# A decoder layer on one core: its 6328 operations put out along one new table over all engines

## The chip, the core and the metric

The kernel runs on one core of one Trainium2 chip. Five engines matter: TensorE for the matrix products (PE, and PEld for its loads of weights into the array), VectorE (DVE), ScalarE (ACT), GpSimd (POOL) and SyncE (SP). SP only issues transfers; POOL issues transfers too and does a few small copies. The metric is the device time of one execution in microseconds, the median over runs. A second time, the span, is that from the first to the last instruction of one profiled execution.

## The reference

One layer of a decoder for 512 tokens of width 1024, all in float32:

```python
u = rms_norm(h, ln_mix_pre)
proj = u @ w_in                  # qa, ka, va | qb, kb, vb | qm | three gates of 1024 columns
y_swa = swa_sink_attention(...)  # 8 heads of 64, 2 key heads, window 128, sinks, T5 bias
y_sb  = stick_breaking_attention(...)          # 8 heads of 64
y_mem = memory_cross_attention(...)            # 4 heads of 128 over 256 memory rows
g = sigmoid(gates)
merged = g0 * (y_swa @ w_branch_swa) + g1 * (y_sb @ w_branch_sb) + g2 * (y_mem @ w_branch_mem)
h = h + rms_norm(merged @ w_out, ln_mix_post)
u = rms_norm(h, ln_ffn_pre)
a = silu(u @ w_gate) * (u @ w_up)              # 2816 columns each
h = h + rms_norm(a @ w_down, ln_ffn_post)
```

In stick-breaking attention a query gives key s the weight beta_s times the product of (1 - beta) over the keys between s and itself.

## The kernel before, in words

*Arithmetic.* A float32 product is made of three products of the kind fp32r (`mm3`): high by high, high by low, low by high. Every operand therefore comes in two parts. `split` makes them: ACT copies the value to the high part (`hi`), then DVE subtracts that from the value (`lo`). Weights come by DMA in blocks of 128 by 1024 (`raw`; where several blocks are summed, `wide`, `ws0p` to `ws2p` and others, partly summed by the DMA itself), are split, and are read by PE. Large projections (gates, branches, gate and up, down) are computed by seven products in place of eight, with sums of blocks formed ahead on DVE, on ACT and by accumulating DMAs, and with sums of results behind (`gp`, `hp`, `seven_*`, `q_*`, `g_*`, `dn_*`).

*Stages.* First x is loaded, gained, split and squared, and the first four weight blocks are loaded in pieces (`first_load`, `first_split`); the sum of squares goes through two products with ones (`rstd_of`: `sh_x`, `sl_x` are the two parts, `on_x` the ones). Then come the projections for the keys, queries and values, the memory's keys and values, the stick-breaking heads (`sb_head`: scores, two sigmoids `bw` and `br`, a scan over the keys on DVE; `sb_turn`: transposes of the weights by products with `c_ident`; `sb_out`: half-array products of the transposed weights `at` with 64 columns of values, two heads making a pair), the window attention (`swa_pair`, transposed weights `pts`, half-array products as well), the branches, `mix`, the turning of the normalized rows (`turn`, transposes again), the gated up and down products (`gu`, `down`) and the closing norm and sum (`dn_half`: `sqr`, `s`, `fg`, then the `out` transfers).

*Two detours through main memory.* The scan is written in differences of successive values, so the values are needed shifted by one row. `next_values` writes them from `v_all` (a part of the buffer named `wide`) to `rows_v`, 1 MB, and loads them back shifted into four buffers `vnext`, 256 KB each; `value_steps` subtracts these on DVE. `band_bias` makes the bias of the window attention, writes it to `bscr`, 1.5 MB, and loads it back skewed into four buffers `bias`. The transfers of both go through POOL's queue.

*Order.* The generator functions put the operations out in an order of their own, with waits where data or buffers need it. Each engine's operations are noted by a helper (line 232 of the kernel, hence the line of nearly all rows of the profile). At the end of `tile_kernel` a literal `ORDER` with one table per engine is laid over them: each operation of an engine is tied behind the one that its table names before it. These ties are of a class without synchronisation (`NoSync`); they only fix the sequence in which the engine takes its work. Between engines the waits come from data and buffers alone.

*Places.* A second literal, `PLAN`, says for every temporary which of the fixed buffers it takes: four each of `raw`, `hi` and `lo`, 45 single buffers and 14 pairs (`ck`, `ck2`), 16 small ones (`s`), and eight PSUM banks of 512 columns (`p`; `p2` takes two banks as one of 1024). `Places.take` deals them out. A transfer or a product that takes a place waits for the last reader of what was there.

*Waits and tables on ACT.* `table` loads a set of activation functions, and each activation is kept behind the load that it needs.

Of the kernel before, what the change touches and what calls it, by code (L numbers as in the profile page):

```python
# [17 lines left out]
P = 128  # L18
# [19 lines left out]
ORDER = {  # L38
    "tensor": (
# [23 lines left out]
    ),  # L63
    "vector": (
# [81 lines left out]
    ),  # L146
}
PLAN = {
    "raw": (
# [2042 lines left out]
```

## Time and profile before

| | |
|---|---|
| median of 3 runs | 768.73 us (768.61 to 768.78) |
| span of the profiled execution | 766.9 us |
| granted TensorE clock | 0.997 on the mean |
| PE busy | 759.1 us, 99% of the span, 4073 instructions |
| DVE busy | 675.2 us, 88%, 1100 |
| ACT busy | 520.3 us, 68%, 946 |
| POOL busy | 104.1 us, 14%, 140 |
| DMA | 150.06 MB, 196 GB/s on the mean |

The median is the time of whole executions; the profiled one is known by its span, and no other time is given for it. The difference of 1.8 us between the two is what lies around the span. A PE instruction is shown as busy for longer than it keeps the next from starting, so what matters for PE is the distance from one start to the next. "Waits" name, for an engine that stood idle, the work that released it.

### The profile page before, as it was taken

How to read it: one execution, taken by the hardware profiler on the slowest of the kernel's cores; microseconds unless marked ns; L12 is line 12 of the kernel's file. 1: busy time of each engine (PE TensorE's matmuls, PEld its weight loads, DVE VectorE, ACT ScalarE, POOL GpSimd, SP SyncE). 2: the span in 40 equal slices, each digit the busy share in tenths (PEclk: the TensorE clock that was granted, in tenths of full speed). 3: DMA queues.
4: the chain of work that ended last, by engine and by line, in shares of the span. 5: the costliest groups of instructions: out<-in, count | busy, mean ns of one | idle time of the engine just before them, and what ended most of it. 6: DMA issues, size and time to landing. Idle time of an engine off the chain costs nothing.

```text
span 766.9 us, 11497 instructions
## 1 busy us (share of the span) xinstructions
PE 759.1 (99%) x4073; PEld 647.3 (84%) x4073; DVE 675.2 (88%) x1100; ACT 520.3 (68%) x946; POOL 104.1 (14%) x140
## 2 busy tenths in 40 slices
PE   9999999999999999999999999999999999999996
PEld 6789888778888888888888899988888888888885
DVE  7994897799989756999897799899999999999966
ACT  7662677777997758677944596566666668957552
POOL 0303242000222110010001201100000000214000
PEclk9999999999999999999999999999999999999998
DMA  8548999734799895469949958876777746859922
GB/s 277 166 142 233 332 328 254 211 111 149 185 188 192 184 203 163 112 134 210 340 128 329 209 130 240 203 191 180 204 192 203 220 142 187 171 120 216 261 75 111
DMA packets 50170, 150.06 MB, mean 196 GB/s; under 512 B 5984, under 2 KB 7952, under 8 KB 50016
## 3 DMA queue, kind: packets, MB, share of 16 engines
q1 hardware_dynamic: 34224, 94.38, 36.8%
q0 software_dynamic: 15600, 54.80, 36.1%
q8 instruction: 32, 0.52, 0.3%
q14 instruction: 26, 0.21, 0.1%
q10 hardware_dynamic: 288, 0.13, 0.1%
HBM read 140.38 MB, written 19.40 MB: 208 GB/s over the span
## 4 chain that ended last, share of the span: by engine, by line
PE 96%; DMA 1%; DVE 1%; ACT 1%; issue 0%; SPq 0%; DVEq 0%
PE bank L232 96%; DMA xT<-in_xT 1%; DMA raw<-in_w_p 0%; DVE xacc L232 0%; SPq L232 0%; ACT pair L232 0%; DVE pair L232 0%; ACT hi L232 0%; ACT xT L232 0%; DVE lo L232 0%; DVE fg L232 0%; DVE sl_x L232 0%; DVEq L2180 0%; DVE s L232 0%; ACT sqr L232 0%
## 5 line engine op out<-in xcount | busy, mean ns | idle before, releaser
L232 PE MATMUL bank<-pair,hi 128*128 128x512 f32 (+1 forms) x1008 | 254.4, 368 | 0.0
L232 DVE TENSOR_TENSOR lo<-raw,hi 128x1024 fp32r<-128x1024 f32 (+4 forms) x149 | 170.7, 1149 | 36.8 <-ACT hi L232 36.2
L232 PEld LDWEIGHTS bank<-pair,hi 128*128 128x128 f32 x1008 | 177.5, 189 | 27.0 <-ACT hi L232 0.9
L232 ACT CAST hi<-raw 128x1024 fp32r<-128x1024 f32 (+4 forms) x149 | 147.7, 998 | 73.7 <-PE bank L232 54.5
L232 PE MATMUL bank<-hi,pair 128*128 128x512 f32 (+1 forms) x628 | 196.3, 374 | 0.0
L232 PE MATMUL bank<-pair,lo 128*128 128x256 f32 (+1 forms) x752 | 154.7, 302 | 0.0
L232 PEld LDWEIGHTS bank<-hi,pair 128*128 128x128 f32 x628 | 115.3, 188 | 19.5 <-issue 0.2
L232 PEld LDWEIGHTS bank<-pair,lo 128*128 128x128 f32 x752 | 115.6, 190 | 10.9 <-DVE lo L232 0.7
L232 PE MATMUL bank<-lo,pair 128*128 128x512 f32 (+1 forms) x330 | 123.6, 375 | 0.0
L232 ACT CAST hi<-wide 128x1024 fp32r<-128x1024 f32 (+1 forms) x61 | 62.2, 1024 | 27.0 <-PE bank L232 11.3
L232 DVE TENSOR_TENSOR lo<-wide,hi 128x1024 fp32r<-128x1024 f32 (+1 forms) x61 | 71.9, 1185 | 4.6 <-ACT hi L232 4.3
L232 PEld LDWEIGHTS bank<-lo,pair 128*128 128x128 f32 x330 | 62.0, 188 | 10.1
L232 POOL DMA_DIRECT2D raw<-in_w_g x24 | 21.1, 878 | 124.4 <-DVE lo L232 106.2
L232 DVE TENSOR_TENSOR gp<-gp,bank 128x512 f32<-128x512 f32 x49 | 33.6, 687 | 4.6 <-PE bank L232 3.7
L232 ACT ACTIVATE sg<-gp 128x256 f32<-128x256 f32 x42 | 17.7, 421 | 23.0 <-DVE gp L232 22.9
L232 POOL DMA_DIRECT2D raw<-in_w_gu x15 | 13.2, 924 | 147.6 <-DMA raw<-in_w_gu 138.5
L232 ACT COPY gp<-bank 128x512 f32<-128x512 f32 x42 | 24.7, 588 | 2.1 <-DVE aq L232 1.4
L232 DVE TENSOR_TENSOR_SCAN bw<-br,bw 128x512 f32<-128x512 f32 (+3 forms) x32 | 24.6, 809 | 0.2
L232 DVE TENSOR_TENSOR gp<-gp,hp 128x512 f32<-128x512 f32 x36 | 24.7, 685 | 0.0
L232 POOL DMA_DIRECT2D wide<-in_w_gu x12 | 11.2, 934 | 84.6 <-DMA wide<-in_w_gu 76.3
L232 ACT COPY hp<-bank 128x512 f32<-128x512 f32 x36 | 21.5, 598 | 0.0
L232 PE MATMUL bank<-hi,ll 128*128 128x512 f32 x50 | 19.4, 389 | 0.0
(624 smaller groups left out, 1371.8 us busy)
## 6 DMA issues: line engine op xcount, KB each, us to landing
wide<-in_w_gu SPq DMA_DIRECT2D x31, 512.0 KB, 5.1
raw<-in_w_gu SPq DMA_DIRECT2D x26, 512.0 KB, 5.4
raw<-in_w_g POOLq DMA_DIRECT2D x24, 512.0 KB, 6.0
raw<-in_w_g SPq DMA_DIRECT2D x18, 512.0 KB, 4.2
raw<-in_w_gu POOLq DMA_DIRECT2D x15, 512.0 KB, 7.2
raw<-in_w_p SPq DMA_DIRECT2D x14, 512.0 KB, 6.3
wide<-in_w_gu POOLq DMA_DIRECT2D x12, 512.0 KB, 5.8
raw<-in_w_brt SPq DMA_DIRECT2D x9, 512.0 KB, 4.8
```

The source lines that it names most:

```text
L232: ins = f(*args, **kw)
```

## The change

The 6328 operations stay the same: 4009 on PE, 1068 on DVE, 876 on ACT, 136 on POOL, 239 on SP, each with the operands of before. What changes:

1. *How they are put out.* The functions of the kernel now only note operations (`Notes`, `Op`); tensors are described by `View` and made when first used (`once`). At the end `Program.put_out` puts out all operations in the order of one table over all engines, and ties each to the one before it on its engine, as before. The code for ordering without a table (`after`, `behind`, `manual_schedule`, high priorities) is gone.
2. *One table in place of five*, drawn up anew. It fixes the same five sequences, but it also fixes how the operations of different engines are interleaved when the program is built.
3. *PLAN drawn up anew*, with the same number of entries of every kind.

```diff
+class Program:
...
+    def put_out(self, nc, order, follow):
+        real = lambda x: x.real() if isinstance(x, View) else x
+        last, out = {}, set()
+        for n in order or range(len(self.ops)):
+            op = self.ops[n]
+            assert all(b.at in out for b in op.behind)
+            out.add(n)
+            args = [real(x) for x in op.args]
+            ins = getattr(getattr(nc, op.engine), op.name)(*args, **{k: real(x) for k, x in op.kw.items()})
+            if op.engine in last:
+                follow(ins, last[op.engine])
+            last[op.engine] = ins
...
-    for e, text in ORDER.items():
-        seen, last = getattr(nc, e).seen, None
...
-                if last is not None:
-                    follow(seen[k], seen[last])
-                last = k
+    order = []
+    for part in ORDER.split():
+        a, _, b = part.partition("-")
+        order += range(int(a), int(b or a) + 1)
+    program.put_out(tc.nc, order, follow)
```

The new table, three pieces from its first part (641 is the write of `rows_v`, 642 to 645 the loads of `vnext`, 646 the write of `bscr`, 760 to 763 the subtracts that read `vnext`, 781 a scan, 824 the first transpose that reads it):

```
... 652 732-733 715 734-736 698 642 747 749 653 752 ...
... 780 790 778 801 760 802 776 803 865 ...
... 844 817 781 818 843 819-821 856 845 763 824 231 822 ...
```

Laid beside the old tables it comes to this:

- On PE 2985 of the 4009 operations stand at another position, by 6 on the mean and by at most 228; the first 13 and the last 12 stand as before. On DVE 1028 of 1068 stand elsewhere, on ACT 795 of 876, on POOL 92 of 136, on SP 217 of 239.
- The transposes stand in 70 runs on PE; before in 42. The half-array products stand in 7 runs; before in 8, since those of the stick-breaking heads 4 to 7 are now back to back. In all runs, before and after, the two products of a pair of heads or halves stand side by side.
- PE's operations that need a fresh wait on another engine, one that an earlier operation of PE has not waited for already, are 529; before 557.
- In the head, the split of the sum of squares of x is followed on PE by five 512-column products of other work and then by the product of its high part, and two places later by that of its low part; before, the two products stood next to each other with no such work ahead. Some low parts of weights come later, and the order of the first products differs accordingly.
- `rows_v` is written and read nearer to its use. Between the write and the first load of `vnext` stand on PE products of 29 times 512, twice 384 and four times 256 columns; between that load and the subtract that reads it 17 times 512, twice 384, four times 256 columns and ten transposes. Behind that subtract DVE has ten operations up to scan 781, and 25 products of 512 columns stand on PE between the subtract and transpose 824. The write of `bscr` stood right behind that of `rows_v`; it now stands behind it by PE work of some 38 us. The shortest distance from the load of a block by POOL to its split is 25 products of 512 columns.
- The loads and sums of `ws0p` and `ws2p` stand later than before.
- Beside the 384 PE operations that took the 80 us from 300 to 380 us before, the table has 126 DVE operations; before 113.
- The first load of an activation table stands at the 40th position on ACT; before at the 3rd. Copies and squares stand ahead of it, and one table load more is then put into the program ahead of them.
- In the tail the last product for `fg` on DVE stands ahead of the last small `s` operation; before behind it.

More of the change, by code (lines that the diff above doesn't have):

```diff
@@ new lines, with __init__, then, __getitem__ @@
+class View:
+    def __init__(self, make, path=(), shape=None):
+        self.make, self.path, self.shape = make, path, shape
+    def then(self, f):
+        return View(self.make, self.path + (f,))
+    def __getitem__(self, k):
+        return self.then(lambda ap: ap[k])
+    def bitcast(self, dt):
+        return self.then(lambda ap: ap.bitcast(dt))
+    def rearrange(self, *args, **kw):
+        return self.then(lambda ap: ap.rearrange(*args, **kw))
+    def unsqueeze(self, axis):
+        return self.then(lambda ap: ap.unsqueeze(axis))
+    def to_broadcast(self, shape):
+        return self.then(lambda ap: ap.to_broadcast(shape))
+    def real(self):
+        ap = self.make()
+        for f in self.path:
+            ap = f(ap)
+        return ap
@@ new lines, with __init__ @@
+class Op:
+    def __init__(self, at, engine, name, args, kw):
+        self.at, self.engine, self.name, self.args, self.kw = at, engine, name, args, kw
+        self.behind = ()
+class Program:
+    def __init__(self):
+        self.ops = []
+    def put_out(self, nc, order, follow):
[10 more added lines that the diff above has]
+            last[op.engine] = ins
+        assert len(out) == len(self.ops)
@@ L256, in __getitem__, with once, f @@
         return self.held[c]
+def once(make):
+    got = []
+    def f():
+        if not got:
+            got.append(make())
+        return got[0]
+    return f
 class Places:
@@ L396, in tile_kernel @@
     places.open(wp, "wide", 1, [P, 5120])
-    cst = first.enter_context(tc.tile_pool(name="cst", bufs=1))
     places.open(sm, "s", 16, [P, 8])
@@ L412, in dps @@
     def dps(name):
-        return places.take(psd, "p" if PLAN else "d", [P, 512], F32, name)
+        return places.take(psa, "p", [P, 512], F32, name)
     def aps(name):
-        return places.take(psa, "p" if PLAN else "a", [P, 512], F32, name)
+        return places.take(psa, "p", [P, 512], F32, name)
     def banks(name):
@@ L425, in split @@
         ins = nc.scalar.copy(hi, raw)
-        lows = nc.vector.tensor_tensor(lo, raw, hi.bitcast(F32), op=ALU.subtract)
-        if "behind" in st:
-            after(ins, st["behind"][0])
-            after(lows, st["behind"][1])
+        nc.vector.tensor_tensor(lo, raw, hi.bitcast(F32), op=ALU.subtract)
         return ins
@@ L441, in w_split @@
         uid[0] += 1
-        hi = places.take(wp, "hi", [P, 1024], F32R, f"hi{uid[0]}", bufs=4)
-        lo = places.take(wp, "lo", [P, 1024], F32R, f"lo{uid[0]}", bufs=4)
+        hi = places.take(wp, "hi", [P, 1024], F32R, f"hi{uid[0]}")
+        lo = places.take(wp, "lo", [P, 1024], F32R, f"lo{uid[0]}")
         if isinstance(raw, list):
             for i, x in enumerate(raw):
-                ins = split(x[:, :], hi[:, i * 512 : (i + 1) * 512], lo[:, i * 512 : (i + 1) * 512])
+                split(x[:, :], hi[:, i * 512 : (i + 1) * 512], lo[:, i * 512 : (i + 1) * 512])
         else:
-            ins = split(raw[:, :n], hi[:, :n], lo[:, :n])
-        if "chain" in st:
-            after(ins, st["chain"])
+            split(raw[:, :n], hi[:, :n], lo[:, :n])
         return hi, lo
@@ L456, in mm3 @@
         (lh, ll), (rh, rl) = l, r
-        one = nc.tensor.matmul(out, lh, rh, start=start, stop=False, skip_group_check=True)
+        nc.tensor.matmul(out, lh, rh, start=start, stop=False, skip_group_check=True)
         nc.tensor.matmul(out, lh, rl, start=False, stop=False, skip_group_check=True)
-        return one, nc.tensor.matmul(out, ll, rh, start=False, stop=stop, skip_group_check=True)
-    def mm3_behind(*args):
-        one, last = mm3(*args)
-        if "products" in st:
-            after(one, st["products"])
-        st["products"] = last
+        nc.tensor.matmul(out, ll, rh, start=False, stop=stop, skip_group_check=True)
     def mm(out, l, r, start, stop):
@@ L474, in tile_kernel @@
     pin, since = [], []
-    def after(ins, first):
-        if not ORDER:
-            follow(ins, first)
     def follow(ins, first):
@@ L486, in fn @@
         ins = nc.scalar.activation(*args, **kw)
-        for p in pin:
-            after(ins, p)
+        ins.behind = tuple(pin)
         since.append(ins)
@@ L494, in table, with const @@
         ins = nc.scalar.preload_act_table_set(name)
-        for x in since:
-            after(ins, x)
+        ins.behind = tuple(since)
         since.clear()
         pin[:] = [ins]
-    def const(name, shape, pool=cst):
-        t = places.fixed(cst, shape, F32, f"c_{name}") if pool is cst else pool.tile(shape, F32, name=f"c_{name}")
+    def const(name, shape, pool=None):
+        t = pool.tile(shape, F32, name=f"c_{name}") if pool else places.fixed(shape, f"c_{name}")
         nc.sync.dma_start(t[:, :], a[name])
@@ L527, in rstd_of @@
         mm(ps[:, :n], one_t[name], l[:, :n], False, True)
-        rb = places.fixed(cst, [P, n], F32, f"rb_{name}")
+        rb = places.fixed([P, n], f"rb_{name}")
         v, t = ck(f"v_{name}"), ck(f"t_{name}")
@@ L533, in rstd_of @@
         nc.gpsimd.dma_start(row[:, :], rb[:1, :])
-        rs = places.fixed(cst, [P, n // P], F32, f"rs_{name}")
+        rs = places.fixed([P, n // P], f"rs_{name}")
         nc.gpsimd.dma_start(rs[:, :], row[:, :].rearrange("o (t p) -> (o p) t", p=P))
@@ L657, in value_steps @@
         for t, x in enumerate(st.pop("vnext")):
-            after(nc.vector.tensor_tensor(own_values(t), own_values(t), x[:, :], op=ALU.subtract), st["scan"])
+            nc.vector.tensor_tensor(own_values(t), own_values(t), x[:, :], op=ALU.subtract)
     def vcols(t, lo):
@@ L971, in gen @@
                 for k in range(2):
-                    mm3_behind(sbank[i][:, :], seven_left(b, p, k, i), cols((hi, lo), k * 512, 512), first and k == 0, last and k == 1)
+                    mm3(sbank[i][:, :], seven_left(b, p, k, i), cols((hi, lo), k * 512, 512), first and k == 0, last and k == 1)
                 yield 1.36
@@ L1210, in tile_kernel @@
-    pin[:] = [first_table]
+    idle = tc.nc.const_aps.tensor(1.0, [P, 512], BF16)
+    one_t = {}
+    for name in ("x", "m"):
+        one_t[name] = ck(f"on_{name}", F32R)[:, :P]
+        nc.vector.tensor_copy(one_t[name], idle[:, :P])
+    pw = dps("warm")
+    for i in range(WARM):
+        mm(pw[:, :], idle[:, :P], idle[:, :], True, True)
+    first_load(nc.scalar, 0, (0, 2))
+    first_table = nc.scalar.preload_act_table_set("natural_log_exp_and_others")
+    pin[:] = [first_table]
+    load_x(0, 1)
@@ new lines, in tile_kernel @@
+    first_load(nc.sync, 0, (1,))
+    load_x(1, 2)
+    first_load(nc.sync, 1, (0, 1))
+    load_x(2, 3)
+    first_load(nc.sync, 1, (2,))
+    first_load(nc.sync, 2, (0,))
+    load_x(3, 4)
+    first_load(nc.sync, 2, (1, 2))
+    load_x(4, 5)
+    first_load(nc.sync, 3)
+    load_x(5, 8)
+    dn.loaded = dn.have = FIRST
+    for p in range(len(PIECE)):
+        for i in range(FIRST):
+            first_split(i, p)
+        for k in range(*PIECE[p]):
+            gain_split(k)
+    xacc = ck("xacc")
@@ new lines, in tile_kernel @@
+    nc.scalar.activation(xacc[:, :], xraw[0][:, :], AF.Square)
+    for k in range(1, KC):
+        nc.scalar.activation(xraw[k][:, :], xraw[k][:, :], AF.Square)
+        nc.vector.tensor_tensor(xacc[:, :], xacc[:, :], xraw[k][:, :], op=ALU.add)
+    dn.ahead(4, 3)
+    for i in range(FIRST):
+        first_ps[("kb", i)] = aps(f"kb{i}")
+    order = [(i, 0, x) for x in ("hh", "lh", "hl") for i in range(FIRST)]
+    order += [(i, 1, x) for i in range(FIRST) for x in ("hh", "lh", "hl")]
+    for i, k, x in order:
+        w = (his if x[0] == "h" else los)[i]
+        mm(first_ps[("kb", i)][:, :], w[:, k * P : (k + 1) * P], u[k][x[1] == "l"], k == 0 and x == "hh", False)
@@ L1212, in tile_kernel @@
+    gens = [dn.units[i]["mm"](his[i], los[i]) for i in range(FIRST)]
+    for k in range(2, KC + 1):
+        for g in gens:
+            next(g, None)
+    dn.at = FIRST
+    st["rs"], st["rb"] = rstd_of("x", xacc, S, aps)
+    for f in st.pop("waiting"):
+        f()
     ident = const("ident", [P, P], base)
-    sinks = places.fixed(cst, [P, 8], F32, "sinks")
+    sinks = places.fixed([P, 8], "sinks")
     nc.sync.dma_start(sinks[:, :], a["sinks"].to_broadcast([P, 8]))
@@ L1985, in tile_kernel @@
     dn.until(f"branch{MEM}")
-    if PLAN:
-        fp = None
-    else:
-        first.close()
-        fp = ctx.enter_context(tc.tile_pool(name="fp", bufs=9, reuse_waits="tile"))
+    fp = wp
     def f_split(raw, n):
         uid[0] += 1
-        hi = places.take(fp, "fhi", [P, 1024], F32R, f"hi{uid[0]}", bufs=4)
-        lo = places.take(fp, "flo", [P, 1024], F32R, f"lo{uid[0]}", bufs=4)
+        hi = places.take(fp, "fhi", [P, 1024], F32R, f"hi{uid[0]}")
+        lo = places.take(fp, "flo", [P, 1024], F32R, f"lo{uid[0]}")
         if isinstance(raw, list):
@@ L2065, in tile_kernel @@
     kept(1)
-    behind(since[-1], st["mixed"])
     table("silu_and_others")
@@ L2075, in tile_kernel @@
     turn_n2(2)
-    behind(*turn_n2(3))
+    turn_n2(3)
     fs.hold = 6
@@ L2079, in tile_kernel @@
     turn_n22(2)
-    behind(*turn_n22(3))
+    turn_n22(3)
     fs.hold = 8
@@ L2083, in tile_kernel @@
     for t in (2, 3):
-        late = turn_late(t, 0)
-    behind(*late)
+        turn_late(t, 0)
     fs.hold = 10
```

297 lines of the change are left out of this document (99 added, 198 removed), and 423 rows, old and new, of tables (ORDER, PLAN).

## The prediction

> **What bounds the kernel now.** I read the span and the busy shares first, then the list of waits, then the chain that ended last.
>
> ```profile
> span 766.9 us, 11497 instructions
> PE 759.1 (99%) x4073; PEld 647.3 (84%) x4073; DVE 675.2 (88%) x1100; ACT 520.3 (68%) x946; POOL 104.1 (14%) x140
> ...
> PE bank L232 <- PEq L2174: 0.8, 1, 0.8
> PE bank L232 <- DVE sl_x L232: 0.4, 1, 0.4
> ...
> 22.29 737.97 PE bank L232 x3990
> 762.87 0.66 DVEq L2180
> ```
>
> The span is 766.9 us. The median of three runs is 768.73 (768.61 to 768.78), so 1.8 us lie around the span. I add the change's terms to the span and give the result plus 1.8. The list of waits has only two entries for PE, the kernel's start and 0.4 us for sl_x. The chain has one piece of 737.97 us, 3990 matmuls in a row, from 22.29 us to 760.3. An order can therefore win only what lies in the holes of that row, the 22 us before it and the 6 us behind it. The holes are found by the distance between starts, since a matmul's own 0.39 us overlaps the next. Three stretches give the prices; the columns are the stretch, its length, busy time and instructions of PE, its weight loads, DVE, ACT and POOL, the granted clock, the share of the DMA engines and GB/s.
>
> ```profile
> 84.00:90.00 6.00, 6.00 (x30) 4.97 (x29) 5.02 (x10) 4.11 (x8) 1.73 (x4) 1.00 1.04 322
> 300.00:380.00 80.00, 80.00 (x385) 66.72 (x384) 73.02 (x113) 62.13 (x114) 7.03 (x8) 1.00 0.71 189
> 700.00:750.00 50.00, 50.00 (x222) 41.40 (x221) 43.02 (x76) 30.41 (x56) 5.42 (x7) 1.00 0.63 167
> ```
>
> In the late stage 222 matmuls take 50.00 us, 0.225 us each at a granted clock of 1.00: the price of a 512-column matmul with nothing in its way. The other two stretches are used below.
>
> **Head holes.** Against that price I lay the starts of the head.
>
> ```profile
> 4.75 1.02 PE L232 MATMUL bank<-pair,hi 128*128 128x512 f32 x3
> 5.61 0.92 PE L232 MATMUL bank<-pair,lo 128*128 128x512 f32 x3
> 6.36 1.30 PE L232 MATMUL bank<-pair,hi 128*128 128x512 f32 x5
> 7.53 0.50 PE L232 MATMUL bank<-pair,lo 128*128 128x512 f32 x1
> 7.87 0.39 PE L232 MATMUL bank<-pair,hi 128*128 128x512 f32 x1
> ...
> 21.54 0.39 PE L232 MATMUL bank<-sh_x,on_x 128*128 128x512 f32 x1
> 22.29 0.50 PE L232 MATMUL bank<-sl_x,on_x 128*128 128x512 f32 x1 [0.37 <-DVE sl_x L232]
> 22.64 0.64 PE L232 MATMUL bank<-pair,hi 128*128 128x512 f32 x2
> ```
>
> From 4.75 to 7.87 stand 12 matmuls in 3.12 us, where 12 x 0.225 is 2.70: 0.4 us of holes. From 21.54 to 22.64 two take 1.10 instead of 0.45: 0.65 us, because the sum of squares (sh_x, sl_x) is multiplied while DVE still subtracts its low part. Together 1.05 us. The new table puts wide products in between: the subtract is followed by five of them (1.1 us) before the first product of the sum. The 0.65 goes whole; what is late next is the same subtract, only if DVE is over 1.1 us behind. Of the 0.40, whose cause is the arrival of x and of the first splits, I take 0.25. Term: **-0.9** (bounds -1.05 and 0; a reordered head can also lose as much as there is of holes, +0.4).
>
> **Holes further on.** The plainest one:
>
> ```profile
> 437.25 0.39 PE L232 MATMUL bank<-pair,hi 128*128 128x256 f32 x1
> 437.47 0.38 PE L232 MATMUL bank<-c_ident,mt 128*128 128x128 f32 x2
> 437.70 0.51 PE L232 MATMUL bank<-pair,hi 128*128 128x256 f32 x2
> ```
>
> A 256-column matmul (half of 0.225) and two transposes (0.11 each, next part) make 0.34; they take 0.45: 0.11 lost. Laying the same prices against all starts of the row of 3990, I estimate 0.66 us of such holes. In the new table the instructions of PE that need a fresh wait on another engine fall from 557 to 529, and results stand further ahead of their readers where they were late here. Term: **-0.5** (-0.66 to 0).
>
> **Transposes and half arrays.** The table draws these runs apart or together, at no change in their number. Transposes (c_ident) stand in 70 runs, before in 42. The price of a change of kind:
>
> ```profile
> 184.25 0.39 PE L232 MATMUL bank<-lo,ys1p5h 128*128 128x512 f32 x1
> 184.49 0.60 PE L232 MATMUL bank<-c_ident,w 128*128 128x128 f32 x4
> 184.84 0.48 PE L232 MATMUL bank<-hi,ys1p5l 128*128 128x512 f32 x1
> 185.16 0.49 PE L232 MATMUL bank<-c_ident,w 128*128 128x128 f32 x3
> 185.40 0.47 PE L232 MATMUL bank<-hi,ys1p5h 128*128 128x512 f32 x1
> 185.71 0.39 PE L232 MATMUL bank<-lo,ys1p5h 128*128 128x512 f32 x1
> ...
> 108.85 0.28 PE L232 MATMUL bank<-kbs,qbl 128*128 128x256 f32 x1
> 109.05 2.38 PE L232 MATMUL bank<-at,wide 128*64 128x512 f32 x16
> 111.36 0.39 PE L232 MATMUL bank<-mh,hi 128*128 128x256 f32 x1
> ```
>
> Two runs of transposes among three wide matmuls take 1.46 us, less 3 x 0.225 leaves 0.785 for seven transposes: 0.112 each, with the changes inside it. Were a bare one half of a 256-column one, 0.056, the changes would cost at most 0.2 a run and 28 more of them 5 us; but the run of four (0.35 from start to start) and that of three (0.24) differ by 0.11, a whole transpose, so no fixed share is left, and I take 0.01 a run, **+0.3** (0 to +0.5). The half-array products (a 128x64 tile of weights, heads of the stick-breaking and window attention) go from 8 groups to 7. Entering one costs 0.20 - 0.11 = 0.09 us by the rows at 108.85 and 109.05, and leaving it, as an estimate, as much again: **-0.2**. Partners of a pair stood side by side in all 8 groups before, so keeping them together buys nothing more.
>
> **The tail.** The last fg product on DVE is put ahead of the last small s operation:
>
> ```profile
> 761.01 0.16 DVE L232 SCALAR_TENSOR_TENSOR s<-s,s 128x1 f32<-128x1 f32 x1 [0.87 <-ACT sqr L232]
> 761.08 0.68 DVE L232 TENSOR_TENSOR fg<-bank,bc_g_fpost 128x512 f32<-128x512 f32 x1
> ```
>
> DVE waits 0.87 us for sqr before s, with the bank that fg reads already complete. The two starts are 0.07 apart, and fg can use the waiting time instead: **-0.1** (-0.6 to 0, since ACT's root and the last products follow).
>
> These five come to -0.9 - 0.5 + 0.3 - 0.2 - 0.1 = -1.4.
>
> **The detour through memory.** The values of the stick-breaking heads go to rows_v in main memory and come back, shifted by a row, as vnext; both are on POOL's queue. Here the tables differ most: bscr, another write on the queue, stands right behind rows_v before, and some 38 us later after; and the loads now stand closer to their use. From the write of rows_v to the first load the new table has matmuls worth 32.5 wide ones, 7.3 us. From there to the DVE subtract that reads it stand 20.5 wide ones and ten transposes, 4.6 + 1.1 = 5.7 us. Together 13.0.
>
> ```profile
> bscr<-brow POOLq DMA_DIRECT2D x1, 1536.0 KB, 15.8
> rows_v<-wide POOLq DMA_DIRECT2D x1, 1024.0 KB, 12.8
> vnext<-rows_v POOLq DMA_DIRECT2D x4, 256.0 KB, 11.8
> raw<-in_w_g POOLq DMA_DIRECT2D x24, 512.0 KB, 6.0
> ...
> DMA to landing us min/median/max: 10.0/11.8/13.7
> ...
> POOL vnext L232 <- DMA rows_v<-wide: 6.0, 1, 6.0
> ```
>
> Today the two take 12.8 + 11.8 = 24.6 us, and POOL stood 6.0 us waiting for the write. At those durations DVE would stand 24.6 - 13.0 = 11.6 us at the subtract. But these landings fall where the 16 DMA engines are full (share 1.04 from 84 to 90 us, window above) with bscr among their load; with bscr gone the nearest row is POOL's other load, 512 KB in 6.0. Bounds: late by 0 and by 11.6. I take the write at 9.4, halfway between 6.0 and 12.8, and the load at 6.0: 15.4, late by 2.4. Behind the subtract DVE has some ten operations up to a scan whose result PE transposes 5.7 us of matmuls later, and DVE is idle for 0.98 of 6.00 us there, so about 0.9 is caught up and the rest stops PE: **+1.5**. Queued behind the waiting subtract are the scans, who make the next attention weights; other loads of POOL wait behind the vnext load, but have 5.7 us or more before their split is wanted.
>
> The Trainium skill, "DMA: Bandwidth & Descriptors", section "Anatomy of one DMA — SWDGE (gpsimd) path", gives a GpSimd-issued transfer 2.0 us plus its bytes at 436 GB/s. By that, an estimate, 1 MB takes 4.4 and 256 KB 2.6 us, and the chain would be there 6 us early, the sum 1.5 lower. The rows, 12.8 and 11.8, disagree while other transfers share the engines.
>
> **DVE where it is fullest.** In the 384 matmuls of 300 to 380 us (window above) DVE has 113 instructions and is busy 73.02 of 80.00 us, 0.646 each. The new table gives DVE 126 instructions beside the same matmuls: 126 x 0.646 = 81.4; with each one's own duration, less the same overlap, I get 79.4. DVE is thus between 0.6 short of full and 1.4 over. Half of the 1.4: **+0.7** (0 to +2). What covers it is banks and splits made ahead of the stretch; if they are gone, PE waits for lo.
>
> **At nothing:** the first activation table on ACT, now 40th in its order instead of 3rd, and one further table load:
>
> ```profile
> L232 ACT ACT_TABLE_LOAD x9 | 11.5, 1283 | 1.8 <-PEq L2174 1.7
> 22.30:80.00 57.70, 57.70 (x322) 52.54 (x323) 45.36 (x71) 28.85 (x44) 15.59 (x29) 1.00 0.65 185
> ```
>
> 1.28 us more on an engine that is busy 28.85 of 57.70 us behind the head; without that cover up to +1.3. The other tables of places keep their counts: only which transfer waits for which buffer's release changes, inside the terms above.
>
> **Sum.** -1.4 + 1.5 + 0.7 = +0.8: span 767.7, time **769.5**. Likeliest case's own range 768.0 to 771.0.
>
> **Rivals.**
> - *The detour is late in full* (the other side). The write still takes 12.8 because weights, not bscr, fill the engines; with the load at 6.0 the chain is 18.8, late by 5.8, less 0.9 caught up: 4.9 instead of 1.5, **772.9**; with the load at 10.0, 776.9. It decides from a DVE wait of about 3 us at the subtract of vnext. For it: the share of 1.04. Against: 1.5 MB less on the queue.
> - *DVE cannot use its idle time at its fullest.* That idle time is mostly a wait for ACT's hi:
>
> ```profile
> L232 DVE TENSOR_TENSOR lo<-raw,hi 128x1024 fp32r<-128x1024 f32 (+4 forms) x149 | 170.7, 1149 | 36.8 <-ACT hi L232 36.2
> ```
>
> 36.8 us over the span are 3.8 in 80. Put on the 1.4 over, 5.2 us pass to PE instead of 0.7: **774.0**. Against: such a wait moves when the order moves.
> - *The detour lands in time.* Its term goes: **768.0**, and **767.3** if DVE keeps up too; with all holes closed 766.8. For it: 1 MB at the pace of POOL's loads would be 9 us or less, and the 256 KB is half of one of them. The skill's rule stands on this side.
> - *The change does nothing measurable,* since PE is busy 99%: part of the forecast.
>
> **How the numbers follow.** Forecast 0.46, detour late in full 0.16, DVE over full 0.13, detour in time 0.25. A measurement here tells about 0.2%, 1.54 us, from no change: faster is below 767.2, slower above 770.3. Faster: 0.11, from the last rival with nearly all holes closed. Same: 0.38 of the forecast and 0.14 of the last rival, 0.52. Slower: 0.08 of the forecast, 0.16 and 0.13: 0.37. The range goes from 766.9, all gains but a little, to 775.0, which takes in the first two rivals' times and leaves out the detour with the load at 10.0.
>
> **What would show it.** Right: no PE wait for sl_x; the chain's row of matmuls begins about 1 us earlier; a DVE wait for vnext of 1 to 3 us and next to it a PE hole before the transposes of bw; DVE over 98% busy in the middle of the run. Wrong: a vnext wait of zero, or of more than 3 us; new entries for PE in the list of waits that name raw's or wide's splits; a longer head; transposes whose changes cost 0.05 us or more a run.

## The result and the profile after

The changed kernel takes 781.6 us (780.2 to 782.1) against 768.75 (768.6 to 769.0) in the same series: 1.0166 times as long, interval 1.0151 to 1.018, or 12.9 us more. I had forecast 769.5, within 766.9 to 775.0. The profiled execution took 781.4 us with a span of 779.6.

The head of the changed kernel's page:

```profile
span 779.6 us, 11580 instructions
...
PE 767.8 (98%) x4073; PEld 642.4 (82%) x4073; DVE 674.4 (87%) x1100; ACT 520.9 (67%) x947; POOL 105.8 (14%) x140
```

The first waits of PE and of its weight loads (us in total, times, longest):

```profile
PE bank L422 <- ACT hi L422: 1.4, 3, 0.8
...
PE bank L422 <- ACT gq1p L422: 0.6, 1, 0.6
...
PEld bank L422 <- ACT hi L422: 3.5, 5, 1.2
...
PEld bank L422 <- DVE pair L422: 1.9, 6, 0.6
PEld bank L422 <- DVE lo L422: 1.5, 7, 0.3
```

And the chain, its shares and its longest piece:

```profile
PE 84%; DVE 6%; DMA 5%; ACT 3%; issue 1%; POOL 0%; SPq 0%; DVEq 0%; ACTq 0%
...
452.59 317.11 PE bank L422 x1770
```

The operations are as before, with one table load more on ACT; what is new is waiting. PE waited for nobody but sl_x; now seven kinds of results stop it, none of them for more than 1.4 us in all, and more kinds stop its weight loads. The row of 737.97 us of matmuls without a break is now 317.11, from 452.59 on. Most of the loss is made up to there, as the next table shows.

I matched every product to itself in the two traces and took how much later PE reaches the same point of its work:

| time in the kernel before, us | 42 | 82 | 123 | 164 | 205 | 246 | 286 | 327 | 367 | 447 | 568 | 760 |
|---|---|---|---|---|---|---|---|---|---|---|---|---|
| changed kernel, late by us | 0.0 | 0.1 | 1.4 | 2.3 | 4.0 | 5.1 | 5.9 | 7.7 | 9.2 | 10.7 | 11.5 | 12.2 |

There is no step in it, only a slope, steepest from 100 to 450 us. One of the larger pieces of the slope, on PE:

```profile
279.54 0.39 PE L422 MATMUL bank<-lo,pair 128*128 128x512 f32 x1
280.37 0.50 PE L422 MATMUL bank<-hi,xsp30h 128*128 128x512 f32 x1 [0.44 <-ACT gq0p L422]
280.71 0.40 PE L422 MATMUL bank<-hi,pair 128*128 128x512 f32 x1
280.95 0.40 PE L422 MATMUL bank<-lo,xsp30h 128*128 128x512 f32 x1
```

From 279.54 to 280.37 are 0.83 us in place of 0.227: a stop of 0.61. The stop also has a tail: the product behind it takes 0.34, the next 0.24. The "idle before" in brackets counts only 0.44, so the distance from start to start is the measure here too. By it the whole run adds up like this, as an estimate with one price for each width: products that start late because a result or a place comes late, 0.9 us in 6 stops before and 8.0 us in 38 stops after (+7.1); products behind those, and the rest of the 512-column ones, 3.0 and 7.4 (+4.4); transposes with their neighbours, 0.9 and 1.5 (+0.6); half arrays, 0.85 and 0.83. Together +12.1, the last number of the table.

Following each of the 38 stops back through what its reader waited for, 8 (3.2 us) begin at a transfer that lands late and 30 (4.7 us) at an earlier product of PE itself, whose result went through ACT and DVE and was not back in time. An example of the second kind, PE, ACT and DVE mixed:

```profile
162.29 0.60 PE L422 MATMUL bank<-at,wide 128*64 128x256 f32 x6
...
162.97 0.59 ACT L422 CAST pair<-bank 128x512 fp32r<-128x512 f32 x1 [1.04 <-PE bank L422]
...
163.45 0.38 ACT L422 COPY yq<-bank 128x256 f32<-128x256 f32 x1
163.86 0.69 DVE L422 TENSOR_TENSOR pair<-bank,pair 128x512 fp32r<-128x512 f32 x1 [1.21 <-ACT yq L422]
...
164.59 0.37 ACT L422 COPY yq<-bank 128x256 f32<-128x256 f32 x1 [0.76 <-DVE pair L422]
165.01 0.38 PE L422 MATMUL bank<-kas,qas 128*128 128x256 f32 x1 [0.26 <-ACT yq L422]
```

The last half-array product ends near 162.9; copy, subtraction and second copy take until 164.96, and PE, which has only 1.75 us of other work in its table in between, stands until 165.01; ACT and DVE stand idle on the way too, each until the other is done (0.76 and 1.21 us). Over the whole run, counted from what each product reads and overwrites in the two programs, products that start less than 0.3 us after the last result or place they need were 30 before and are some 160 after, of 4000; the median of that margin falls from some 7 to some 5 us.

And the first kind, the chain of the changed kernel:

```profile
265.61 8.41 DMA raw<-in_w_g
...
281.94 0.89 POOL ws2p L422
282.83 15.80 DMA raw<-in_w_g
298.65 1.06 ACT hi L422
```

The second of these weight blocks of 512 KB took 15.80 us; the median of these loads on POOL was 6.0 and is 7.4. ACT, which never waited for in_w_g before, now does:

```profile
ACT hi L422 <- DMA raw<-in_w_g: 15.9, 10, 3.3
```

The new table puts sums of weights (ws0p, ws2p) between these loads. The stages, changed kernel, columns as in the windows of the prediction:

```profile
20.00:62.00 42.00, 42.00 (x216) 36.80 (x215) 30.95 (x51) 22.25 (x34) 8.51 (x14) 1.00 0.47 152
104.00:146.00 42.00, 41.79 (x261) 33.79 (x260) 39.64 (x64) 31.29 (x60) 5.99 (x8) 1.00 0.72 213
251.00:313.00 62.00, 61.35 (x278) 49.64 (x277) 46.56 (x58) 45.29 (x68) 12.08 (x15) 1.00 0.99 255
313.00:376.00 63.00, 62.05 (x295) 49.98 (x294) 62.00 (x99) 50.11 (x97) 7.02 (x8) 1.00 0.80 214
```

and the same work in the kernel before:

```profile
20.00:62.00 42.00, 41.63 (x213) 36.19 (x212) 39.78 (x61) 26.11 (x41) 7.97 (x17) 1.00 0.51 152
104.00:144.00 40.00, 40.00 (x258) 32.59 (x257) 34.55 (x57) 28.34 (x56) 10.38 (x15) 1.00 0.99 282
246.00:306.00 60.00, 60.00 (x277) 49.96 (x276) 40.50 (x51) 41.92 (x63) 7.00 (x8) 1.00 0.79 194
306.00:367.00 61.00, 61.00 (x297) 51.12 (x296) 59.27 (x92) 43.98 (x82) 7.03 (x8) 1.00 0.68 156
```

Three things changed place. DVE does less from 20 to 62 us (51 instructions, before 61) and more later. The transfers' share falls from 0.99 to 0.72 at 104 to 144 us and rises from 0.79 to 0.99 at 251 to 313. And DVE is full from 313 to 376 us, 62.00 of 63.00.

### The profile page after: what moved, and what is told of

Its sections match the earlier page's. It is cut to its first block, busy times and chain, and to the rows that moved or that the text cites. A ratio compares the mean times of both kernels' runs of the same rounds, so it can differ in the third digit from the quotient of the medians.

```text
span 779.6 us, 11580 instructions
## 1 busy us (share of the span) xinstructions
PE 767.8 (98%) x4073; PEld 642.4 (82%) x4073; DVE 674.4 (87%) x1100; ACT 520.9 (67%) x947; POOL 105.8 (14%) x140
## 4 chain that ended last, share of the span: by engine, by line
PE 84%; DVE 6%; DMA 5%; ACT 3%; issue 1%; POOL 0%; SPq 0%; DVEq 0%; ACTq 0%
PE bank L422 84%; DMA raw<-in_w_g 3%; DVE lo L422 1%; DMA raw<-in_w_brt 1%; ACT hi L422 1%; DVE pair L422 1%; DMA xT<-in_xT 1%; ACT pair L422 0%; DVE yq L422 0%; ACT w L422 0%; DVE fg L422 0%; DVE w L422 0%; ACT mt L422 0%; DVE s L422 0%; ACT yq L422 0%
## 5 line engine op out<-in xcount | busy, mean ns | idle before, releaser
L422 PE MATMUL bank<-pair,hi 128*128 128x512 f32 (+1 forms) x1016 | 262.3, 369 | 1.0 <-ACT hi L422 0.4
L422 PE MATMUL bank<-hi,pair 128*128 128x512 f32 (+1 forms) x730 | 221.5, 378 | 0.2 <-ACT hi L422 0.2
L422 PE MATMUL bank<-pair,lo 128*128 128x256 f32 (+1 forms) x760 | 159.4, 302 | 0.0
L422 PEld LDWEIGHTS bank<-hi,pair 128*128 128x128 f32 x730 | 133.9, 188 | 25.5 <-ACT hi L422 0.9
L422 PE MATMUL bank<-lo,pair 128*128 128x512 f32 (+1 forms) x372 | 137.7, 378 | 0.0
L422 PEld LDWEIGHTS bank<-pair,lo 128*128 128x128 f32 x760 | 119.4, 190 | 11.0 <-DVE lo L422 0.2
L422 PEld LDWEIGHTS bank<-lo,pair 128*128 128x128 f32 x372 | 69.7, 188 | 12.7 <-DVE lo L422 1.1
L422 DVE TENSOR_TENSOR_SCAN bw<-br,bw 128x384 f32<-128x384 f32 (+3 forms) x32 | 25.2, 813 | 0.5 <-ACT br L422 0.2
L422 PE MATMUL bank<-pair,pair 128*128 128x512 f32 (+2 forms) x76 | 24.0, 379 | 0.0
L422 POOL DMA_DIRECT2D raw<-in_w_gu x11 | 9.6, 875 | 99.2 <-DMA raw<-in_w_gu 99.2
```

The lines of the kernel that those rows point to most:

```text
L422: ins = getattr(getattr(nc, op.engine), op.name)(*args, **{k: real(x) for k, x in op.kw.items()})
```

## The experiments

Operation numbers in the edits are those of the tables. Times are medians; before is 768.6 to 768.7 in all series. "Late by" is measured as in the table above.

**Machinery or tables?** The new code for putting out, with the old sequences merged into its one table, and the old places:

```diff
-ORDER = ( new table )            PLAN = { new places }
+ORDER = ( the five old ones )    PLAN = { old places }
```

> The new way of putting out, with the old five sequences merged into one table in the order of their starts in the trace of before, and the old table of places. If the loss lies in the tables (sequences and places), 768.7 us, within 0.5 of before. If it lies in how the program is put out (other waits between the engines, one more table load), 775 to 781.

768.68 us (768.27 to 768.98), ratio 1.000 (0.999 to 1.0009). The code is neutral; sequences and places together carry all 12.9 us.

**Banks.** Of the 38 late starts 20 wait for a place. By the places that the program deals out, PSUM bank 1 is idle from 45 to 198 us, and bank 7 is not used before 299 us. So the changed kernel with its PSUM banks dealt out anew over all eight:

```diff
-    "p": "0 1 0 2 4 3 5 6 4 6 2 5 ..."
+    "p": "0 1 2 3 5 4 6 7 0 5 2 3 ..."      (191 of 215 entries)
```

> The changed kernel with only the PSUM banks dealt out anew: the new table leaves bank 1 unused from 45 us and bank 7 unused to some 300 us; here each product takes the free bank that was released longest ago, 191 of 215 entries differ. Bank theory: 20 of the 38 holes of PE (4.1 us, and about 1.9 of slow restarts behind them) end with a bank's release and go, 781.6 becomes 775 to 777.5. Engine theory (DVE and ACT are late anyway, and PE would stop a few products later for their results): 780 to 781.5.

780.75 us, ratio 1.0161 (1.0143 to 1.0179). The stops for a place fall from 20 (4.1 us) to 8 (2.3), but those for a result of DVE rise from 13 (2.1) to 20 (5.4). PE meets the same lateness further on. The banks are where half of it showed; dealing them out better does not bring the loss back.

**DVE's early debt.** DVE has done 11 us less work than before when PE reaches 42 us. Four kernels give stretches their old order: DVE, ACT and POOL from 20 to 62 us (a2); all engines old up to 62 us and new behind (c_before62), or new up to 62 or 246 us and old behind.

> The changed kernel with DVE, ACT and POOL in the stretch 20 to 62 us in the sequence of before: the root of the sum of squares and the scaling of the keys and queries ahead of the splits that wait for a place; the first table load in 3rd position again. DVE theory (the 8.8 us of work that DVE does not do by 62 us keep it without reserve up to about 190 us, and PE stops for it): holes between 84 and 190 us, 4 us, mostly go, 777 to 778.5. Bank theory or transfer theory: 781, no more than 0.7 gained in the head.

> Old sequences of all engines for everything that before had started by 62 us, the new ones for the rest. Debt theory (what DVE leaves undone in the first 62 us is paid where PE stops for it later): the lag of about 3.3 us that the changed kernel gathers from 84 to 190 us mostly goes, 777.5 to 779, although the stretch up to 62 us itself costs the changed kernel only 0.1 us. Local theory (each stretch loses by its own sequences): 781 to 781.6.

> New sequences for everything that the changed kernel had started by 62 us, the old ones for the rest. Debt theory: DVE starts the second part some 9 us of work behind, and PE stops for it before 190 us: 771 to 773. Local theory: 768.7 to 769.3.

> New sequences up to 246 us of the changed kernel, the old ones behind. Both theories: what the changed kernel lost by then, 5 us, stays: 773.5 to 774. If the loss behind 246 us (7 us) comes from what the earlier part left undone, and not from the later sequences, more: 776 to 781.

787.5, 805.4, 796.9 and 809.4 us. None is clean, because places had to be redrawn at each seam and PE then waited for them (behind 246 us for 24 us on one result of ACT, which stood 25 us itself for a weight load). What can be read lies away from the seams. With DVE, ACT and POOL in their old order from 20 to 62 us PE loses some 4 us from 82 to 205 us, as the changed kernel does. With the old order of all engines up to 62 us the new one loses 6.1 us from 80 to 200 us, more than its own 3.9: paying the debt early does not help it. With the new order up to 62 us the old one pays the debt at once and then loses 0.1 us from 82 to 205 us. So the slope goes with the new order of the middle, as far as runs with redrawn places can tell, and not with its beginning.

**DVE's amount of work.** The low part of a split as a plain copy, so that the subtraction and its wait for ACT's copy are left out, in the changed kernel and in that before:

```diff
-        nc.vector.tensor_tensor(lo, raw, hi.bitcast(F32), op=ALU.subtract)
+        nc.vector.tensor_copy(lo, raw)
```

> The changed kernel with the low parts of all splits made by a copy of the value (so they are wrong) in place of the subtraction of the high part: DVE has less work per split and no longer waits for ACT there. Theory of late DVE: with DVE relieved, most holes that end with DVE go (13 that end with a result and 11 that end with a bank, 4.1 us, and about 2 of restarts behind them), 774 to 776.5; what ends with ACT and with late weights stays. If the distances between a product and the product that depends on it are too short by themselves, through ACT as well: 779 or more.

> The kernel before with the low part of each split made by a plain copy of the raw tile in place of the subtraction (the low parts are then the raw values, a part of the computation that is left out). It is the counterpart of the run in which the changed kernel had the same. Theory (amount of work on DVE is not what sets either kernel's time): DVE's busy time falls from 674 us to about 553 us and the time stays: 768.4 to 768.8. Rival (DVE, 88 per cent busy, holds PE up in both): 766 or less.

779.64 us (ratio 1.0147, 1.0132 to 1.0162) and 768.08 (0.9993, 0.9984 to 1.0002). Busy shares of the first:

```profile
PE 765.2 (98%) x4073; PEld 643.4 (83%) x4073; DVE 552.8 (71%) x1100; ACT 519.2 (67%) x947; POOL 109.7 (14%) x140
```

and the largest wait of its DVE:

```profile
DVE lo L422 <- PE bank L422: 57.0, 49, 6.9
```

122 us of work less on DVE bring 2 us; DVE waits for PE's release of places instead. Its capacity does not set the time. The kernel before gains 0.5 us, which its times can't tell from nothing; in its trace PE is 0.6 us ahead from 40 us to the end, about the hole for sl_x.

**More room on PE.** 276 positions of PE drawn so that products stand further behind what they need, on top of the new banks; then also the weight sums (next experiment) moved:

> The changed kernel with all eight banks (as in a1_banks) and with PE's sequence alone eased: where a product would wait for ACT or DVE, up to 30 places further on one that is ready is taken first; 276 positions of PE differ, the sequences of the other four engines are those of the change. Distance theory (the new tables put a product too few products behind the one that it depends on by way of ACT and DVE, and PE's sequence is part of that): 776 to 778. If the holes come from how late ACT and DVE are in their own sequences, whatever PE does: 780 to 781.

> As f_banks_pe, with the sums of ws2p and ws0p on POOL's queue put forward as in a3_ws; PE's sequence is eased anew for that. If the three causes add up: 1 to 2 us less than f_banks_pe, 774 to 776.5. If each removes only what the next then stops: 779 to 781.

782.57 and 781.11 us: no gain, where the theory of short distances on PE had 776 to 778. In the first PE is 0.2 us early at 123 us, where the changed kernel is 1.4 late, but 8.8 late at 286: stops that begin at a transfer grow from 8 (3.2 us) to 20 (6.6), those that begin at PE fall from 30 (4.7) to 13 (2.8). In the second it is 6 (2.6) and 20 (3.8). What is gained at one kind of reader is lost at the next queue, and PE's own sequence alone does not hold the loss.

**The sums of weights.** In the changed kernel 14 transfers of POOL (ws0p4 to ws0p7, ws2p4 to ws2p7) taken out from between the loads of in_w_g, back to 140 us on:

```diff
 # POOL, changed kernel
-... 867 868 1647 1731 975 909 976 910 1817 1005 ... 1071 2187 1072 2207 ...
+... 867 868 1071 909 1100 1072 910 1101 975 1151 976 1152 1005 1168 1006 1169 1647 1731 1817 ...
```

> The changed kernel with only 14 transfers on POOL's queue (the sums of ws2p and the later half of those of ws0p) put forward to the quiet stretch from 140 us on. Transfer theory (they fill the DMA engines from 200 to 310 us, and the weights that POOL and SP load beside them come after they are wanted): ACT's waits for in_w_g, 15.9 us, go below 4, the holes of PE at 240, 280 and 300 us go, 778 to 779.5; no hole ahead of 200 us changes. Bank or DVE theory: 781 to 781.6.

780.66 us (ratio 1.016, 1.0139 to 1.018), about 1 us less, within the spread. ACT's wait for these loads falls from 15.9 to 8.7 us,

```profile
ACT hi L426 <- DMA raw<-in_w_g: 8.7, 8, 2.7
```

stops that begin at a transfer from 8 (3.2 us) to 3 (1.3), and in the profiled run, the fastest of its four, PE ends 10.0 late in place of 12.2.

The reverse: the same 14 transfers put between the loads in the kernel before, no place redrawn.

```diff
 # POOL, kernel before
-... 867 909 1071 1100 868 910 1072 1101 641 646 975 ... 1169 799 ... 1817 1731 1755 ...
+... 867 868 641 646 ... 799 800 1647 1817 1731 975 909 976 910 1005 1755 ... 1071 2187 1072 2207 ...
```

> The kernel before with one edit: the 14 transfers on POOL that sum the weights ws0p4 to ws0p7 and ws2p4 to ws2p7 stand where the changed kernel has them, between the loads of in_w_g (from 205 to 310 us instead of 64 to 142), with no place drawn otherwise. Theory (the sums beside the weight loads are a cost of their own): POOL's loads of in_w_g, 5.4 to 6.5 us before, take 8 to 15 us, ACT waits for DMA raw<-in_w_g for 5 to 15 us where the kernel before shows none, and PE loses 1 to 3 us between 230 and 330 us: 769.7 to 771.7, nearest 770.9 (the 2.2 us by which the changed kernel's profiled lag shrank when they were taken out). Rival (the sums cost only beside the changed kernel's thin margins): ACT's wait appears, PE's doesn't, 768.5 to 768.9.

791.87 us (787.3 to 793.0), ratio 1.0292 (1.027 to 1.0314): 23 us from fourteen transfers whose sums are not read before 286 us in the kernel before. I had expected 2. The profiled run is the fastest of the five, 787.3 us, and PE ends 18.6 us late in it; the other four took 790.9 to 793.0. Waits of PE, ACT and DVE:

```profile
PE bank L416 <- DVE pts L416: 5.9, 1, 5.9
PE bank L416 <- ACT wide L416: 2.8, 1, 2.8
...
ACT xsp30h L416 <- DMA xq<-xq: 13.3, 1, 13.3
...
DVE pts L416 <- DMA xq<-xq: 7.2, 1, 7.2
```

POOL in order of time:

```profile
212.60 0.84 POOL L416 DMA_DIRECT2D ws0p<-in_w_brt  x1 [5.51 <-DMA ws0p<-ws0p]
...
218.85 0.51 POOL L416 DMA_DIRECT2D ws0p<-ws0p  x1 [4.17 <-PE bank L416]
219.39 1.80 POOL L416 DMA_DIRECT2D xq<-xq  x2
```

and PE at the second stop:

```profile
298.89 0.28 PE L416 MATMUL bank<-mks0l,qms0h 128*128 128x256 f32 x1
302.02 0.79 PE L416 MATMUL bank<-hi,pair 128*128 128x512 f32 x1 [2.85 <-ACT wide L416]
302.61 0.63 PE L416 MATMUL bank<-lo,pair 128*128 128x512 f32 x1
303.04 1.05 PE L416 MATMUL bank<-hi,pair 128*128 128x512 f32 x2
```

A sum adds onto an earlier transfer, so POOL stands 5.51 us until that has landed (the chain of that run ends the second stop too, 4.17 us, with the landing of such a sum, at 218.38 us), and the xq transfers queued behind start late; ACT and DVE stand for them, and PE for DVE. From 287 us on two weight loads take 12.7 and 16.2 us beside ws2p. So the sums are dear where the queue has no slack for them. The new tables ask for xq later (its split xsp30h starts at 235.3 us, before at 223.2), and ACT has no such wait there: that fits with a gain of 1 us and not 20 where the sums are taken out, though no run moves xq alone. I had priced them from the changed kernel alone.

**One engine's new sequence alone.** No run has a compute engine's whole new sequence beside the old others. This one has POOL's, with 117 places redrawn.

> The kernel of before (old sequences on PE, DVE, ACT and SP, old places but for some single buffers) with the new sequence on POOL alone: rows_v and vnext, bscr, bias and the sums of ws0p and ws2p in the order of the change. Transfer theory: POOL's new order by itself makes weights late, ACT waits 5 us or more for in_w_g, 770.5 to 772.5. If the old sequences have the reserve for it: 768.4 to 769.3.

817.67 us, ratio 1.0638 (1.0624 to 1.0653), far above both expectations. Half a table is worse than either whole one; how much of the 49 us the redrawn places cost, and how much the moved weight sums of the experiment above, this run does not part.

**One edit that should gain.** The product of sl_x, which PE waits for at 22.29 us, three products later in the kernel before; first with 97 places redrawn by the way, then with none.

```diff
 # PE
-... 167 168 206 207 208 209 ...
+... 167 206 207 208 168 209 ...
```

> The kernel of before with one product moved: the second product of the sum of squares of x (sl_x) stands three products later, as the change spaces it. The hole of 0.5 us at 21.5 us goes, 0.12 of the restart behind it too: 768.1 (0.4 to 0.6 less). If the root of the sum, which comes later by that, stops DVE's scaling of the keys: 768.6 to 769.

> The kernel before (its five sequences and its places, put out by the new machinery, which alone took 768.68 against 768.62) with one edit: the product of sl_x and on_x stands three products later on TensorE, and not one of the 5,000 places is drawn otherwise. An earlier run of the same edit had places redrawn by the way and lost 2.2 us at a single buffer. Theory (an edit to a table is worth what its own hole was, if the places stay): the hole of 0.53 us at 22.3 us and its restart of about 0.1 go, no new one comes: 768.1 us, ratio 0.9992. Rival (PE's wait only moves on, as it did in the runs with banks and weights changed): another hole of 0.3 to 0.6 us in the next 20 us, 768.6 us, ratio 1.000.

770.84 us (ratio 1.0035, 1.0023 to 1.0047), and 768.37 (0.9997, 0.9988 to 1.0006). In the first PE is 0.3 to 0.5 us ahead from 40 to 600 us, then loses it all and more at one single buffer, still read by a transfer of h. PE and ACT there:

```profile
645.67 1.11 PE L414 MATMUL bank<-pair,lo 128*128 128x256 f32 x8
648.82 0.96 PE L414 MATMUL bank<-pair,hi 128*128 128x512 f32 x3 [2.03 <-ACT hp L414]
```

```profile
648.18 0.58 ACT L414 COPY hp<-bank 128x512 f32<-128x512 f32 x1 [3.28 <-DMA h<-xr]
```

One place drawn badly, of 1,686 (not 5,000, as the expectation has it), costs 2.2 us. With the places kept, PE stays 0.7 us ahead to its end in the profiled run; in the times that is 0.26 us, which this measurement can't tell from nothing.

**The length of the round trip.** Weight splits, all but the first of them and a few of other shapes, on every fourth column only, in both kernels; order, places, waits and transfers stay.

```diff
-            split(raw[:, :n], hi[:, :n], lo[:, :n])
+            k = 4 if uid[0] > 40 else 1
+            split(raw[:, :n:k], hi[:, :n:k], lo[:, :n:k])
```

> The changed kernel with the splits of weights (all but the first of them) on every fourth column only, on ACT and on DVE alike; the other columns of the high and low parts keep what lay in the place before, so a part of the computation is left out. Order, places, waits and transfers are the changed kernel's. A copy of 128x1024 takes 0.998 us on ACT and the subtraction 1.149 on DVE; at a quarter of the elements I expect 0.3 to 0.4 each, so that a round trip of copy and subtraction shrinks from about 2.2 to 0.7 us and a place comes free 1.5 us sooner. Theory (most of the 12.9 us are round trips from PE over ACT and DVE back to PE, drawn too short in the new sequences): the 30 stops that begin at an earlier product and most of their restarts go, the 8 that begin at a transfer are halved, 770 to 773 us, ratio 1.002 to 1.006. Rival (the transfers on POOL and the order of the queues hold the rest): 777 to 780, and the list of waits still names ACT hi behind DMA raw<-in_w_g.

> The same thinning of the weight splits (every fourth column, the rest left out) in the kernel before, as a control: it shows what cheaper splits bring where few results are late. Theory and rival alike: its holes by late results are 0.9 us in all, 768.0 to 768.7 us.

775.33 us (ratio 1.0089, 1.0072 to 1.0105) and 768.23 (0.9996, 0.9986 to 1.0005). The thinned copies and subtractions, by form:

```profile
L422 ACT CAST hi<-raw 128x256 fp32r<-128x256 f32 x126 | 81.4, 652 | 65.3 <-PE bank L422 32.3 <-DMA raw<-in_w_g 20.2 <-DVE raw L422 9.0
L422 DVE TENSOR_TENSOR lo<-raw,hi 128x256 fp32r<-128x256 f32 x126 | 77.5, 619 | 34.3 <-ACT hi L422 23.3 <-PE bank L422 9.6 <-ACT gq2p L422 0.5
```

They take 0.65 and 0.62 us, not 0.3 to 0.4. Whole blocks of 1024 columns take 1.06 and 1.22 (the 0.998 and 1.149 of the expectation are means over several shapes), so the round trip shrinks from 2.28 to 1.27 us. Of the 12.9 us 6.3 go; the kernel before gains 0.4 at most. The stops fall from 38 (8.0 us) to 22 (4.5), and PE ends 6.1 us late; from 286 us on it loses 1.6 us more, where the changed kernel loses 6.3. It lands between the two theories: half of the loss goes when weight splits are shorter. That is the time that a weight block spends between its landing or its place's release and its first product, but ACT and DVE also have 63 and 94 us less to do. Less work on DVE alone brought 2 us above; less work on ACT alone was not tried, so the two readings are not wholly parted. In the other half are round trips without a weight split (the stop at 165.01 us above is unchanged, 0.42 us), transfers, and the tails of the stops.

**What stays open.** Sequences and places were not tried apart in full; so how the 12.9 us divide between them is not settled. Nor do I have a version that is measurably faster than the kernel before.

## Why the prediction was wrong, point by point

- *Head, -0.9.* The wait for sl_x is gone, as said. The first splits come later instead, as "a longer head" allowed for: at 20 us PE is 0.7 late, at 42 us level. Net 0.0. The term took the gain and not its counterpart.
- *Holes further on, -0.5.* This is the step that failed. I argued that PE's operations that need a fresh wait fall from 557 to 529, and that results stand further ahead where they were late. A count of waits says nothing on margins. The holes of this kind grew from 0.9 to 8.0 us, because products now start less than 0.3 us behind what they need at some 130 more places; with the tails that is +11.5, against a bound of 0. The order of all products was there to be read before: the work on PE between a product and the reader of its result through ACT and DVE, less the durations of those steps and of what is queued ahead of them, gives each margin. I laid out that distance for the vnext detour alone.
- *Transposes, +0.3.* +0.6, by 0.022 us a run for the 0.01 I took; just above the bound of 0.5. *Half arrays, -0.2:* 0.0.
- *Detour, +1.5.* Zero. There is no DVE wait for vnext, and it was "a vnext wait of zero" that should count against me:

```profile
rows_v<-wide POOLq DMA_DIRECT2D x1, 1024.0 KB, 6.0
vnext<-rows_v POOLq DMA_DIRECT2D x4, 256.0 KB, 5.4
```

  6.0 + 5.4 = 11.4 us stand against 13.0 of cover. The write took half of its 12.8. The term laid that on bscr, and the runs do not bear it out: in the kernel before with only the 14 weight sums moved away, bscr is still issued 1.65 us behind rows_v, and the write takes 4.8, the loads 10.7:

```profile
rows_v<-wide POOLq DMA_DIRECT2D x1, 1024.0 KB, 4.8
vnext<-rows_v POOLq DMA_DIRECT2D x4, 256.0 KB, 10.7
```

  So the weight sums held the write up, the transfers that I had put at nothing. The estimates by the Trainium skill, "DMA: Bandwidth & Descriptors", section "Anatomy of one DMA — SWDGE (gpsimd) path", were 4.4 and 2.6 us; they stood on the right side, and the measured 6.0 and 5.4 exceed them.
- *DVE at its fullest, +0.7.* DVE is busy 62.00 of 63.00 us there, 98.4%, as said, and PE loses about 2.2 us beside it (7.0 to 9.2 in the table's terms from 306 to 367 us), 1.0 of it at a late weight at 372 us. That is near the upper bound of 2, but DVE's being full is not what costs it. With the light low part DVE is busy only 51.38 us in the same window, and PE loses 2.1 us there all the same:

```profile
313.00:376.00 63.00, 61.99 (x296) 50.35 (x296) 51.38 (x101) 50.16 (x98) 7.44 (x8) 1.00 0.79 217
```

  So the size came out by luck, and the mechanism is not borne out.
- *At nothing: the tables of places, "inside the terms above".* The weight sums moved beside the weight loads were listed in the change and not priced. They hold part of 8 stops, 3.2 us, and can cost 23 where nothing covers them. What the new places cost by themselves stays open.
- *The tail, -0.1.* PE ends 12.2 us late and the span is 12.7 longer: it lost 0.5.
- *The rivals.* "Lands in time" was right on the detour, wrong in time, and its "9 us or less" for 1 MB does not follow from its row: 512 KB in 6.0 makes 12 us for twice as much, less only if part of the 6.0 does not grow with the size; "detour late" and "DVE over full" each named one wait. None was the sum of many small ones, which was the case. The entries for PE in the list of waits that name splits, given as a sign of a wrong prediction, are what came.

## What to carry to other kernels

When a whole order is drawn anew on an engine that is 99% busy, price it over the whole table: for every product the margin between the end of what it needs and its turn, and every transfer that changes its neighbours on a queue. This kernel lost a little at many places, and none of the single repairs tried here got it all back; most of what was gained at one wait was lost at the next. Change such a table one operation at a time with all places kept, and take its gain only if the next hundreds of microseconds stay level.

## What the runs showed of the hardware

- A stop of PE costs more than its length, with the granted clock at 1.00. After one of 0.1 us or more, the next 512-column product takes 0.34 us from start to start in place of 0.227, on the mean of ten in the changed kernel 0.106 us more, and the following ones about 0.24.
- After a longer stop the clock falls. Behind the gap from 298.89 to 302.02 us with the moved weight sums, products stand 0.43 us apart until 305.2, then 0.23 again, and the granted clock of that stretch is halved at first:

```profile
302.00:306.00 4.00, 3.98 (x11) 3.19 (x12) 1.94 (x3) 0.46 (x1) 0.00 (x0) 0.58 1.02 346
```

  Seven products take 3.15 us there for 1.59, so 1.56 us are lost on top of the gap of 3. The length of the gap alone does not decide it. In the run with POOL's new sequence the clock is halved behind a gap from 761.51 to 763.63 us and a shorter one after it, and stays whole around a gap from 301.74 to 304.11:

```profile
300.00:308.00 8.00, 6.02 (x27) 4.63 (x26) 5.75 (x6) 5.43 (x7) 2.68 (x3) 1.00 0.84 226
764.70:768.00 3.30, 3.11 (x7) 2.51 (x8) 3.30 (x6) 0.96 (x2) 0.00 (x0) 0.50 1.08 310
```

  No stop of the changed kernel, 1.0 us at most, halved it. The Trainium skill, "TensorE: Matmul & The Clock Gate", section "Part 1: The HAM clock gate", has the clock at half after at least one idle window of about 3.4 us, and whole again after about 3.4 us of work. Here gaps of 3.1 and of 2.1 us were enough, and the slow stretch behind the first lasted 3.2.
- A copy of a quarter of the elements, at a stride of four, took 0.65 us where the whole takes 1.06 on ACT, and 0.62 of 1.22 on DVE. A copy of 256 columns that lie side by side takes 0.37 (the row at 164.59), but it reads a PSUM bank and makes no fp32r, so the stride is not the only difference.
